# Gate and up of nine of eleven feature pairs by seven half-size products, and the down projection in four groups

## The chip, the cores and the metric

The kernel runs on one core of one Trainium2 chip. The metric is the device time of one execution in microseconds. Before the change it is 1094.81 us, the median of three runs (1094.68 to 1096.13). One execution was profiled as well; all rows below are from it.

The core has five engines with a queue of instructions each, worked off in order and tied together by semaphores: TensorE (PE in the rows, its weight loads PEld), VectorE (DVE), ScalarE (ACT), GpSimd (POOL) and SyncE (SP), which here only issues DMAs. SBUF is the working memory with 128 partitions, PSUM the matmuls' memory with eight banks.

## The reference

Two transformer layers over 512 tokens of width 1024, in float32. Layer A mixes tokens by a gated short convolution and attention to 256 memory tokens, layer B by sliding-window attention and the same memory. Each ends in a feed-forward part of width 2816:

```python
x = x + jnp.concatenate([y_tok, y_mem], axis=-1) @ w_out
h = rmsnorm(x, norm_ffn[i])
x = x + (jax.nn.silu(h @ w_gate[i]) * (h @ w_up[i])) @ w_down[i]
...
return rmsnorm(x, final_norm)
```

## The kernel before, in words

Features lie on the partitions, in blocks of 128: x has 8 blocks, the feed-forward 22, and a block spans all 512 tokens. Weights and activations are split into a high part (a cast on ScalarE, L95) and a low part (source minus high part on VectorE, L96), and `mm3` (L88 to L92) adds three matmuls, high by high, high by low and low by high. `project` (L320) makes one block of outputs from all blocks of inputs in one PSUM bank: 8 x 3 matmuls of 512 columns for gate or up, 22 x 3 for down.

Weights come in tiles of 128 x 1024 in the order of their use (`weight_order`), loaded on SP's queue and split two tiles ahead (`AHEAD`). Raw tiles have two buffers of their own, high and low parts three each, and the softmax tiles three; all other wide tiles share 31.

The feed-forward part (`ffn_up`, L543) goes through the 22 blocks: gate, 1/rms on VectorE (`times_r`, L278), Silu on ScalarE (L551), up, 1/rms, then the product of both on GpSimd (L555), and its split into h. `ffn_down` then makes the eight blocks of x from all 22 h; `residual` (L521) adds each to x and prepares the next norm. In layer B the last of the eight blocks is made by halves of the tokens (256 columns), so that one half is finished behind the other's products. The order on each engine is the order in which the code issues the work; small pieces of attention and norms are issued some steps later by `Background`.

Of the kernel before, what the change touches and what calls it, by code (L numbers as in the profile page):

```python
# [15 lines left out]
P = 128  # L16
D = 1024
# [19 lines left out]
NB = S // P  # L37

# blocks of the concatenated mixer outputs, in the order in which they appear
# [19 lines left out]
def yoco_kernel(ctx: ExitStack, tc: tile.TileContext, io: dict):  # L59
# [3 lines left out]
    wraw = ctx.enter_context(tc.tile_pool(name="wraw", bufs=2))  # L63
    wspl = ctx.enter_context(tc.tile_pool(name="wspl", bufs=3))
# [23 lines left out]
    def mm3(out, w, x, first, last):  # L88
        """out += w^T x from exact two-part splits; w, x = (hi, lo)."""
        nc.tensor.matmul(out, lhsT=w[0], rhs=x[0], start=first, stop=False)  # L90
        nc.tensor.matmul(out, lhsT=w[0], rhs=x[1], start=False, stop=False)  # L91
        nc.tensor.matmul(out, lhsT=w[1], rhs=x[0], start=False, stop=last)  # L92
# [30 lines left out]
    def weight_order():  # L123
        def mem_kv(i):
# [7 lines left out]
        def ffn(i):  # L132
            for f in range(KF):
                yield io["w_gate"][i, f]
                yield io["w_up"][i, f]
            for m in range(KD):
                for c in range(0, KF, 8):
                    yield io["w_down"][i, m][:, c * P:min(c + 8, KF) * P]
# [672 lines left out]
```

## Time and profile before

| | before |
|---|---|
| median of three runs | 1094.81 us |
| profiled execution, span from first to last instruction | 1092.4 us |
| TensorE, VectorE, ScalarE, GpSimd busy | 1075.7, 587.2, 423.7, 188.1 us |
| matmuls of 512 columns, of 256 columns | 4238, 628 |
| moved by DMA | 108.66 MB |

The page gives one execution's span and no time around it; the median of the runs is 2.4 us longer. Busy time counts the recorded duration of instructions. Matmuls are recorded from start to modelled end and overlap, so the distance from one start to the next is what a matmul takes of TensorE. The counts of matmuls are from the program's order, the rest from the page.

### The profile page before, as it was taken

What the parts mean: (1) busy time and instruction counts of PE and PEld (TensorE: products, weight loads), DVE (VectorE), ACT (ScalarE), POOL (GpSimd) and SP (SyncE); (2) the same over time, 40 slices, a digit from 0 to 9 for tenths busy, and PEclk for the clock granted to TensorE, in tenths of its full rate; (3) what the DMA queues carried; (4) which work ended last, traced back from release to release, by engine and by line L of the source; (5) the groups of instructions that cost most, each with busy time, mean ns of one, the idle gap of its engine ahead of it and who ended that gap; (6) DMA issues with size and microseconds to landing.
All of it is one profiled execution on the core that took longest, in us unless ns stands there. A gap on an engine that the chain in (4) does not pass through costs nothing. (4 is left out here: it accounts for less than half of the span.)

```text
span 1092.4 us, 13009 instructions
## 1 busy us (share of the span) xinstructions
PE 1075.7 (98%) x5152; PEld 902.2 (83%) x5152; DVE 587.2 (54%) x782; ACT 423.7 (39%) x700; POOL 188.1 (17%) x143
## 2 busy tenths in 40 slices
PE   9999999999999999999999999999999999999996
PEld 7788988888888888888888887888888888888886
DVE  7587856454545454333369798744545454532223
ACT  6346634332323232223258687543323233322220
POOL 5331202210101010000012133330101010100000
PEclk9999999999999999999999999999999999999998
DMA  7323233223232323333351222132232323233222
GB/s 224 125 97 115 77 127 106 89 86 110 86 111 84 111 86 102 87 98 100 105 174 59 92 63 70 44 130 96 82 112 85 108 89 105 89 95 105 88 87 77
DMA packets 34036, 108.66 MB, mean 99 GB/s; under 512 B 3852, under 2 KB 7864, under 8 KB 33848
## 3 DMA queue, kind: packets, MB, share of 16 engines
q1 hardware_dynamic: 31840, 103.82, 29.4%
q10 hardware_dynamic: 2136, 4.01, 1.3%
q8 instruction: 40, 0.66, 0.2%
q14 instruction: 20, 0.16, 0.1%
HBM read 105.71 MB, written 4.47 MB: 101 GB/s over the span
## 5 line engine op out<-in xcount | busy, mean ns | idle before, releaser
L95 ACT CAST whi<-raw 128x1024 fp32r<-128x1024 f32 (+2 forms) x196 | 199.4, 1018 | 508.5 <-PE p_u L91 168.6
L96 DVE TENSOR_TENSOR wlo<-raw,whi 128x1024 fp32r<-128x1024 f32 (+2 forms) x196 | 287.8, 1469 | 182.1 <-ACT whi L95 181.4
L555 POOL TENSOR_TENSOR fu<-fg,fu 128x512 f32<-128x512 f32 x44 | 58.1, 1320 | 412.2 <-ACT whi L95 268.5
L91 PE MATMUL p_d<-h,whi 128*128 128x512 f32 x330 | 128.4, 389 | 0.0
L90 PE MATMUL p_d<-h,whi 128*128 128x512 f32 x330 | 128.4, 389 | 0.0
L92 PE MATMUL p_d<-h,wlo 128*128 128x512 f32 x330 | 128.4, 389 | 0.0
L90 PEld LDWEIGHTS p_d<-h,whi 128*128 128x128 f32 x330 | 61.9, 188 | 13.0
L91 PEld LDWEIGHTS p_d<-h,whi 128*128 128x128 f32 x330 | 61.9, 188 | 12.9
L92 PEld LDWEIGHTS p_d<-h,wlo 128*128 128x128 f32 x330 | 61.9, 188 | 12.7
L90 PE MATMUL p_u<-xoa,whi 128*128 128x512 f32 x176 | 68.6, 390 | 0.0
L90 PE MATMUL p_u<-xob,whi 128*128 128x512 f32 x176 | 68.6, 390 | 0.0
L90 PE MATMUL p_g<-xoa,whi 128*128 128x512 f32 x176 | 68.5, 389 | 0.0
L90 PE MATMUL p_g<-xob,whi 128*128 128x512 f32 x176 | 68.5, 389 | 0.0
L92 PE MATMUL p_g<-xoa,wlo 128*128 128x512 f32 x176 | 68.5, 389 | 0.0
L92 PE MATMUL p_g<-xob,wlo 128*128 128x512 f32 x176 | 68.5, 389 | 0.0
L91 PE MATMUL p_g<-xoa,whi 128*128 128x512 f32 x176 | 68.5, 389 | 0.0
L91 PE MATMUL p_g<-xob,whi 128*128 128x512 f32 x176 | 68.5, 389 | 0.0
L92 PE MATMUL p_u<-xoa,wlo 128*128 128x512 f32 x176 | 68.5, 389 | 0.0
L92 PE MATMUL p_u<-xob,wlo 128*128 128x512 f32 x176 | 68.5, 389 | 0.0
L91 PE MATMUL p_u<-xoa,whi 128*128 128x512 f32 x176 | 68.5, 389 | 0.0
L91 PE MATMUL p_u<-xob,whi 128*128 128x512 f32 x176 | 68.5, 389 | 0.0
L278 DVE TENSOR_TENSOR fu<-p_u,rb_fb 128x512 f32<-128x512 f32 x22 | 15.2, 691 | 69.5 <-PE p_u L92 69.5
(321 smaller groups left out, 2079.0 us busy)
## 6 DMA issues: line engine op xcount, KB each, us to landing
raw<-in_w_gate SPq DMA_DIRECT2D x44, 512.0 KB, 3.5
raw<-in_w_up SPq DMA_DIRECT2D x44, 512.0 KB, 3.5
raw<-in_w_down SPq DMA_DIRECT2D x32, 512.0 KB, 3.5
raw<-in_a_w_in SPq DMA_DIRECT2D x14, 512.0 KB, 3.5
raw<-in_w_down SPq DMA_DIRECT2D x16, 384.0 KB, 3.1
raw<-in_a_w_out SPq DMA_DIRECT2D x8, 512.0 KB, 3.4
raw<-in_b_w_q SPq DMA_DIRECT2D x8, 512.0 KB, 3.5
raw<-in_b_w_out SPq DMA_DIRECT2D x8, 512.0 KB, 3.4
```

The costliest lines, as they stand in the source:

```text
L90: nc.tensor.matmul(out, lhsT=w[0], rhs=x[0], start=first, stop=False)
L91: nc.tensor.matmul(out, lhsT=w[0], rhs=x[1], start=False, stop=False)
L92: nc.tensor.matmul(out, lhsT=w[1], rhs=x[0], start=False, stop=last)
L95: nc.scalar.copy(out=hi, in_=src)
L96: nc.vector.tensor_tensor(out=lo, in0=src, in1=hi.bitcast(F32), op=ALU.subtract)
L278: nc.vector.tensor_tensor(out=t, in0=acc, in1=norm.row, op=ALU.mult)
L555: nc.gpsimd.tensor_tensor(out=u, in0=t, in1=u, op=ALU.mult)
```

## The change

Features are taken in pairs of blocks, eleven of them. Two pairs (`PLAIN`) are computed as before, except that VectorE instead of GpSimd multiplies gate and up. For the other nine, gate and up are one unit each: the product of [two output blocks x 1024 inputs] with [1024 inputs x 512 tokens] is cut into quarters (inputs in even and odd blocks, tokens in two halves of 256) and computed by seven products of quarter size for eight, in Winograd's form of Strassen's identity. Four of the seven weight operands are sums of quarters (t1 to t4), made by `minus`; four of the activations' are sums too (s1 to s4). `XForms` makes all activations' operands once per layer, after normalising x fully on VectorE, and splits them into high and low parts. `Unit` loads a unit's weights, makes and splits its operands and issues the products; partial sums leave PSUM by way of ScalarE copies (`self.r`) and VectorE additions (`evacuate`). For w11 and w21 the low part is made by ScalarE writing the negated high part and an accumulating DMA on GpSimd's queue adding the weights from DRAM to it.

`Queue` runs a clock of matmul times as the code is issued, and `work.at` puts every step of a unit at a time relative to its first product: the load 16 products ahead, and so on. The down projection is made in four groups of pairs (`SPLITS`), each added to x; the last group of layer B has its last two blocks by halves of the tokens. The buffers of raw and split weights and of the softmax move into one pool of 41 wide tiles (`DBUFS`). Comments are left out of the diff.

```diff
+DBUFS = 41
+PLAIN = 2
+SPLITS = ((0, 1), (2, 3, 4), (5, 6, 7), (8, 9, 10))
+def mm_time(n):
+    return n / 2400 + 0.0135
+SLOT = 3 * NJ * mm_time(H)
...
-        return slots.tile([P, 2, S], dt, tag="d", name=name, bufs=31)
+        return slots.tile([P, 2, S], dt, tag="d", name=name, bufs=DBUFS)
...
     def probs(name):
-        """Softmax tile, [queries, block of queries, 256 keys]."""
-        t = slots.tile([P, 2, S], F32, tag="p", name=name, bufs=3)
+        t = wide(name, F32)
...
+        def pump(self):
+            while self.items and self.items[0][0] <= self.now:
+                heapq.heappop(self.items)[2]()
...
+    def mm3(out, w, x, first, last, reopen=False):
+        work.now += 3 * mm_time(out.shape[-1])
+        nc.tensor.matmul(out, lhsT=w[0], rhs=x[0], start=first, stop=False, skip_group_check=reopen)
+        nc.tensor.matmul(out, lhsT=w[0], rhs=x[1], start=False, stop=False, skip_group_check=reopen)
+        nc.tensor.matmul(out, lhsT=w[1], rhs=x[0], start=False, stop=last, skip_group_check=reopen)
...
+        def down(i, s):
+            k0, k1 = 2 * SPLITS[s][0], 2 * SPLITS[s][-1] + 2
+            yield from (io["w_down"][i, m][:, k0 * P:k1 * P] for m in range(KD))
...
+            raw, hi, lo = (wide(f"{t}{n}", dt).rearrange("p a b -> p (a b)")[:, :w]
+                           for t, dt in (("raw", F32), ("whi", FR), ("wlo", FR)))
...
+    XFORM = {1: "x11", 2: "x12", 3: "s4", 4: "x22", 5: "s1", 6: "s2", 7: "s3"}
+    WFORM = {1: "w11", 2: "w21", 3: "w22", 4: "t4", 5: "t1", 6: "t2", 7: "t3"}
...
+        def group(self, jj):
+            d = {}
...
+            def normed(k):
+                if k % 4 == 0:
+                    d["e"], d["o"] = (wide(f"xn{self.name}{c}{jj}", F32) for c in "eo")
+                nc.vector.scalar_tensor_tensor(out=d["eo"[k % 2]][:, k % 4 // 2, :], in0=x[k], scalar=gain(self.g, k),
+                                               in1=self.norm.row, op0=ALU.mult, op1=ALU.mult)
+                self.normed += 1
...
+            def combine(out, a, b, op):
...
+                nc.vector.tensor_tensor(out=d[out], in0=d[a], in1=d[b], op=op)
...
+            def divide(f):
+                t = wide(f"xf{self.name}{f}{jj}")
+                hi, lo = (t[:, z, :].rearrange("p (k t) -> p k t", t=H) for z in range(2))
+                split(d[f], hi, lo)
+                self.t[f, jj] = t
...
+            yield from (lambda k=k: normed(k) for k in range(4 * jj, 4 * jj + 4))
+            yield lambda: divide("x11")
+            yield lambda: combine("s1", "x21", "x22", ALU.add)
+            yield lambda: combine("s2", "s1", "x11", ALU.subtract)
+            yield lambda: divide("x12")
+            yield lambda: combine("s3", "x11", "x21", ALU.subtract)
+            yield lambda: combine("s4", "x12", "s2", ALU.subtract)
+            yield from (lambda f=f: divide(f) for f in ("s2", "s1", "s3", "x22", "s4"))
...
+            def load():
+                for c in range(2):
+                    d[c] = flat(f"raw{name}{c}", F32)
+                    nc.sync.dma_start(out=d[c], in_=src[:, 2 * c * W:2 * (c + 1) * W])
...
+            def plain():
+                hi, lo = flat(f"hi{name}a", FR), flat(f"lo{name}a", FR)
+                nc.scalar.copy(out=hi, in_=d[0])
+                nc.scalar.activation(lo, hi.bitcast(F32), AF.Copy, scale=-1.0)
+                nc.gpsimd.dma_start(out=lo, in_=src[:, :2 * W], accum_op=ALU.add)
+                halves(hi, lo, ("w11", "w21"))
...
+            def w22():
+                t = wide(f"w22{name}")
+                self.w["w22"] = t[:, 0, :], t[:, 1, :]
+                split(d["w22"], *self.w["w22"])
...
+            def minus(out, a, b):
+                nc.vector.tensor_tensor(out=d[out], in0=d[a], in1=d[b], op=ALU.subtract)
...
+            def high(c):
+                d["hi", c] = flat(f"hi{name}t{c}", FR)
+                nc.scalar.copy(out=d["hi", c], in_=d[c])
+            def low(c, names):
+                lo = flat(f"lo{name}t{c}", FR)
+                nc.vector.tensor_tensor(out=lo, in0=d[c], in1=d["hi", c].bitcast(F32), op=ALU.subtract)
+                halves(d["hi", c], lo, names)
...
+            for slot_, fn in (
+                    (-16, load), (-8, plain), (-6.5, w22), (-5.5, lambda: minus("w12", "w12", "w11")),
+                    (-5, lambda: minus("w22", "w22", "w12")), (-4, lambda: high(1)),
+                    (-3, lambda: low(1, ("t2", "t1"))), (-1.5, lambda: minus("w11", "w22", "w11")),
+                    (-1, lambda: minus("w21", "w21", "w22")), (0, lambda: high(0)),
+                    (1, lambda: low(0, ("t3", "t4")))):
+                work.at(t0 + slot_ * SLOT, fn)
...
+        def product(self, k, xf):
...
+            b = {1: "a", 6: "a", 7: "a", 4: "a", 2: "b", 5: "c", 3: "c"}[k]
+            opens = k in (1, 2, 5)
+            if opens:
+                self.bank[b] = ps(f"{b}{self.name}")[:, :H]
+            for j in range(NJ):
+                w = tuple(t[:, j * P:(j + 1) * P] for t in self.w[f])
+                mm3(self.bank[b], w, xf.part(XFORM[k], j), opens and j == 0, j == NJ - 1,
+                    not opens)
+                work.pump()
+            self.done.add(k)
+            if k in (1, 6, 7):
+                self.r[k] = slot(f"r{k}{self.name}", F32, H)
+                nc.scalar.copy(out=self.r[k], in_=self.bank["a"])
+            if k == 2:
+                self.evacuate(0, 0, self.bank["b"], self.r[1])
+            if k == 4:
+                self.evacuate(0, 1, self.bank["a"], None)
+            if k in (5, 7) and {5, 7} <= self.done:
+                self.evacuate(1, 1, self.bank["c"], self.r[7])
+            if k == 3:
+                self.evacuate(1, 0, self.bank["c"], self.r[6])
+            bg.tick()
...
+        def gate(f, e, bank, r):
+            to = quarter(g, f, e)
+            def silu(src):
+                nc.scalar.activation(to, src, AF.Silu)
+                gated.add((f, e))
+            if r is None:
+                silu(bank)
+                return
+            nc.vector.tensor_tensor(out=to, in0=bank, in1=r, op=ALU.add)
+            work.after(0.9, lambda: silu(to))
...
+        def up(f, e, bank, r):
+            work.until(lambda: (f, e) in gated)
+            to, by = quarter(u, f, e), quarter(g, f, e)
+            if r is not None:
+                nc.vector.tensor_tensor(out=to, in0=bank, in1=r, op=ALU.add)
+                bank = to
+            nc.vector.tensor_tensor(out=to, in0=bank, in1=by, op=ALU.mult)
+            count[f] += 1
+            if count[f] == 2:
+                hi, lo = pair_of(f"h{i}_{2 * p + f}")
+                work.after(0.8, lambda: nc.scalar.copy(out=hi, in_=u[:, f, :]))
...
+                def low():
+                    nc.vector.tensor_tensor(out=lo, in0=u[:, f, :], in1=hi.bitcast(F32), op=ALU.subtract)
+                    h[2 * p + f] = hi, lo
+                work.after(1.6, low)
...
+        count = [0, 0]
+        return [Unit(io["w_gate4"][i, p - PLAIN], t0, f"g{i}_{p}", gate),
+                Unit(io["w_up4"][i, p - PLAIN], t0 + 7 * SLOT, f"u{i}_{p}", up)]
...
+    def down(h, blocks, name):
+        early = len(blocks) - 2
+        acc, w = [], []
+        for m in range(2):
+            w.append(next(weights))
+            acc.append(ps(f"{name}{m}"))
+            for k in range(early):
+                mm3(acc[m], cols(w[m], k), h[blocks[k]], k == 0, False)
+                work.pump()
+                if k % 2:
+                    bg.tick()
+        work.until(lambda: all(b in h for b in blocks))
+        for m in range(2):
+            for k in range(early, len(blocks)):
+                mm3(acc[m], cols(w[m], k), h[blocks[k]], k == 0, k == len(blocks) - 1)
+            work.pump()
+            bg.tick()
+            yield m, acc[m]
+        for m in range(2, KD):
+            yield m, project([h[b] for b in blocks], f"{name}{m}", len(blocks))
...
+    def ffn(i, xg, norm, g):
...
+        for s in range(1, len(SPLITS)):
+            work.at(downs[s] - 7, weights.open)
+            for n, p in enumerate(SPLITS[s]):
+                units[p] = ffn_units(i, p, starts[s] + 14 * n * SLOT, h)
...
+        for f in range(2 * PLAIN):
             pg = project(xg, f"g{i}_{f}")
...
-            nc.gpsimd.tensor_tensor(out=u, in0=t, in1=u, op=ALU.mult)
+            if f == 0:
+                xf = XForms(norm, g, f"{i}", 1.25)
+            nc.vector.tensor_tensor(out=u, in0=t, in1=u, op=ALU.mult)
             hi, lo = pair_of(f"h{i}_{f}")
             split(u, hi, lo)
-            h.append((hi, lo))
+            h[f] = hi, lo
...
+        for s in range(len(SPLITS)):
+            prev = None
+            todo = [u for p in SPLITS[s] if p >= PLAIN for u in units[p]]
+            for u in todo:
+                order = [(u, 1), (u, 2), (prev, 4), (u, 6), (prev, 3)]
+                order += [(u, 7), (u, 5), (u, 4), (u, 3)] if u is todo[-1] else [(u, 5), (u, 7)]
+                for v, k in order:
+                    if v is not None:
+                        v.product(k, xf)
+                prev = u
+            if s < len(SPLITS) - 1:
+                work.until(lambda: xf.normed == KD)
+                for m, acc in down(h, blocks_of(s), f"d{i}{s}_"):
+                    nc.vector.tensor_tensor(out=x[m], in0=acc, in1=x[m], op=ALU.add)
+                for b in blocks_of(s):
+                    del h[b]
         return h
...
-    def ffn_down(i, h, norm, g):
-        return [residual(m, project(h, f"d{i}_{m}", KF), norm, g, f"xd{i}") for m in range(KD)]
...
+    LAST = len(SPLITS) - 1
...
+    h = ffn(0, xg, nF, G_FFN0)
...
+    xg = [residual(m, acc, nB, G_MIX1, "xd0") for m, acc in down(h, blocks_of(LAST), "d0_")]
...
+    w = {m: next(weights) for m in (KD - 2, KD - 1)}
+    blocks = blocks_of(LAST)
+    for t0 in (0, H):
+        for m in (KD - 2, KD - 1):
+            acc = ps(f"d1_{m}_{t0}")[:, :H]
+            for n, b in enumerate(blocks):
+                mm3(acc, cols(w[m], n), tuple(a[:, t0:t0 + H] for a in h[b]), n == 0, n == len(blocks) - 1)
...
```

Three places of the order. The first is VectorE in the gate and up products of layer A, in the kernel before (block 18 to 19: `fg` and `fu` are gate and up after 1/rms, `wlo` a weight tile's low part, `h` the low part of h).

```order
L278 TENSOR_TENSOR fg_18_3107<-p_g_18_3076,rb_fa 128x512
L96 TENSOR_TENSOR wlo_3113<-raw_3111,whi_3112 128x1024
L278 TENSOR_TENSOR fu_18_3141<-p_u_18_3110,rb_fa 128x512
L96 TENSOR_TENSOR wlo_3150<-raw_3148,whi_3149 128x1024
L96 TENSOR_TENSOR h_18_3144<-fu_18_3141,h_18_3144 128x512
L278 TENSOR_TENSOR fg_19_3178<-p_g_19_3147,rb_fa 128x512
L96 TENSOR_TENSOR wlo_3184<-raw_3182,whi_3183 128x1024
L278 TENSOR_TENSOR fu_19_3212<-p_u_19_3181,rb_fa 128x512
L96 TENSOR_TENSOR wlo_3221<-raw_3219,whi_3220 128x1024
L96 TENSOR_TENSOR h_19_3215<-fu_19_3212,h_19_3215 128x512
```

The same place in the change, where pair 9 follows pair 8 (`rawg`, `rawu` are weights in which sums are made in place, `log`, `lou` low parts, `g`, `u` the evacuated quarters, `r7`, `r1` partial sums that ScalarE copied).

```order
L761 TENSOR_TENSOR g_9_1793<-cg_9_4586,r7g_9_4617 128x256
L697 TENSOR_TENSOR rawg_101_4497<-rawg_101_4497,rawg_100_4495 128x512
L768 TENSOR_TENSOR u_9_1794<-bu_9_4641,r1u_9_4639 128x256
L770 TENSOR_TENSOR u_9_1794<-u_9_1794,g_9_1793 128x256
L705 TENSOR_TENSOR lou_9t_4683<-rawu_90_4370,hiu_9t_4665 128x1024
L135 TENSOR_TENSOR w22g_10_4673<-rawg_101_4497,w22g_10_4673 128x512
L697 TENSOR_TENSOR rawu_101_4626<-rawu_101_4626,rawu_100_4624 128x512
L697 TENSOR_TENSOR rawg_101_4497<-rawg_101_4497 128x512
L761 TENSOR_TENSOR g_9_1793<-cg_9_4586,r6g_9_4567 128x256
L697 TENSOR_TENSOR rawg_100_4495<-rawg_101_4497,rawg_100_4495 128x512
L697 TENSOR_TENSOR rawg_100_4495<-rawg_100_4495,rawg_101_4497 128x512
L705 TENSOR_TENSOR log_10t_4730<-rawg_101_4497,hig_10t_4715 128x1024
```

Two weight splits, two scalings and the split of h per block have become, per unit, four sums of weights, three splits and the additions and multiplications of quarters, interleaved by their times.

The second place is TensorE where one block of outputs follows another, before (from up of block 3 to gate of block 4 in layer A; the waits are those that the program writes down).

```order
L91 MATMUL p_u0_3_2045<-xoa_7_1779,whi45_1976 128x512
L92 MATMUL p_u0_3_2045<-xoa_7_1779,wlo45_1977 128x512
L90 MATMUL p_g0_4_2082<-xoa_0_1608,whi46_2013 128x512 [waits Activation_49]
L91 MATMUL p_g0_4_2082<-xoa_0_1608,whi46_2013 128x512
L92 MATMUL p_g0_4_2082<-xoa_0_1608,wlo46_2014 128x512 [waits DVE_49]
L90 MATMUL p_g0_4_2082<-xoa_1_1613,whi46_2013 128x512
L91 MATMUL p_g0_4_2082<-xoa_1_1613,whi46_2013 128x512
```

In the change, where the gate unit of pair 4 begins (`au0_3` is a bank of the up unit of pair 3, `ag0_4` of the gate unit of pair 4, `xf` an operand of the activations).

```order
L129 MATMUL au0_3_2680<-xf0s31_2168,hiu0_3t0_2725 128x256
L130 MATMUL au0_3_2680<-xf0s31_2168,hiu0_3t0_2725 128x256
L131 MATMUL au0_3_2680<-xf0s31_2168,lou0_3t0_2743 128x256
L129 MATMUL ag0_4_2805<-xf0x110_1918,hig0_4a_2706 128x256
L130 MATMUL ag0_4_2805<-xf0x110_1918,hig0_4a_2706 128x256
L131 MATMUL ag0_4_2805<-xf0x110_1918,log0_4a_2707 128x256 [waits DMASW4_49]
L129 MATMUL ag0_4_2805<-xf0x110_1918,hig0_4a_2706 128x256
L130 MATMUL ag0_4_2805<-xf0x110_1918,hig0_4a_2706 128x256
```

The bank's first product waits at its third matmul for a DMA of GpSimd's queue (DMASW), where before a weight tile's cast and subtraction were waited for.

The third place is TensorE at the end of the plain pairs in layer A, before at the last h block of the down projection (`h0_21`, after 63 matmuls of that block of outputs).

```order
L90 MATMUL p_d0_0_3363<-h0_20_3286,whi84_3365 128x512
L91 MATMUL p_d0_0_3363<-h0_20_3286,whi84_3365 128x512
L92 MATMUL p_d0_0_3363<-h0_20_3286,wlo84_3366 128x512
L90 MATMUL p_d0_0_3363<-h0_21_3357,whi84_3365 128x512 [waits Activation_49]
L91 MATMUL p_d0_0_3363<-h0_21_3357,whi84_3365 128x512 [waits DVE_49]
L92 MATMUL p_d0_0_3363<-h0_21_3357,wlo84_3366 128x512
```

In the change the first group has four h blocks, and the last of them (`h0_3`) comes after 18 matmuls on the others.

```order
L129 MATMUL d00_1_2177<-h0_2_2058,whi47_2104 128x512
L130 MATMUL d00_1_2177<-h0_2_2058,whi47_2104 128x512
L131 MATMUL d00_1_2177<-h0_2_2058,wlo47_2105 128x512
L129 MATMUL d00_0_2161<-h0_3_2152,whi46_2063 128x512 [waits Activation_49]
L129 MATMUL d00_1_2177<-h0_3_2152,whi47_2104 128x512
L130 MATMUL d00_0_2161<-h0_3_2152,whi46_2063 128x512 [waits DVE_49]
L131 MATMUL d00_0_2161<-h0_3_2152,wlo46_2064 128x512
L130 MATMUL d00_1_2177<-h0_3_2152,whi47_2104 128x512
L131 MATMUL d00_1_2177<-h0_3_2152,wlo47_2105 128x512
```

The wait for the last h block, for ScalarE's high part and VectorE's low part, stands 18 matmuls after the last up product instead of 63.

## Rows read from the trace of the kernel before

**Rows 1.** The page: span, busy engines, TensorE and its granted clock in 40 slices.

```profile
span 1092.4 us, 13009 instructions
PE 1075.7 (98%) x5152; PEld 902.2 (83%) x5152; DVE 587.2 (54%) x782; ACT 423.7 (39%) x700; POOL 188.1 (17%) x143
...
PE   9999999999999999999999999999999999999996
...
PEclk9999999999999999999999999999999999999998
```

**Rows 2.** Table of stretches: us, busy of each engine (instructions), granted clock, DMA.

```profile
60.00:190.00 130.00, 130.00 (x696) 112.51 (x695) 94.16 (x131) 66.89 (x123) 28.37 (x17) 1.00 0.33 109
190.00:435.00 245.00, 245.00 (x1088) 202.95 (x1088) 122.17 (x114) 76.29 (x94) 32.65 (x24) 1.00 0.29 95
435.00:560.00 125.00, 125.00 (x553) 103.05 (x552) 40.99 (x45) 36.31 (x45) 10.85 (x8) 1.00 0.33 98
560.00:720.00 160.00, 154.53 (x885) 132.63 (x884) 132.91 (x286) 113.18 (x270) 46.80 (x36) 1.00 0.28 91
720.00:960.00 240.00, 240.00 (x1066) 198.89 (x1065) 119.59 (x111) 74.33 (x91) 30.87 (x23) 1.00 0.29 95
```

**Rows 3.** Waits of TensorE, longest in total first: us, times, longest.

```profile
PE v L90 <- DVE kf L278: 1.7, 1, 1.7
PE pt_s L325 <- DVE den_s L650: 1.1, 1, 1.1
```

**Rows 4.** Timeline of TensorE, feed-forward of layer A: start, duration, instruction.

```profile
300.95 0.39 PE L90 MATMUL p_u<-xoa,whi 128*128 128x512 f32 x1
...
306.39 0.39 PE L90 MATMUL p_g<-xoa,whi 128*128 128x512 f32 x1
```

**Rows 5.** Timeline of TensorE in the last block, and that stretch's row.

```profile
1075.72 0.28 PE L90 MATMUL d<-h,whi 128*128 128x256 f32 x1
...
1079.20 0.28 PE L92 MATMUL d<-h,wlo 128*128 128x256 f32 x1
...
1069.50:1079.30 9.80, 9.80 (x84) 9.80 (x83) 0.42 (x1) 0.42 (x1) 0.00 (x0) 1.00 0.01 2
```

**Rows 6.** Timeline of VectorE, feed-forward of layer A; in brackets the idle time before.

```profile
307.50 2.33 DVE L96 TENSOR_TENSOR wlo<-raw,whi 128x1024 fp32r<-128x1024 f32 x1 [0.21 <-ACT whi L95]
309.75 0.68 DVE L96 TENSOR_TENSOR h<-fu,h 128x512 fp32r<-128x512 f32 x1
312.03 0.69 DVE L278 TENSOR_TENSOR fg<-p_g,rb_fa 128x512 f32<-128x512 f32 x1 [1.60 <-PE p_g L92]
312.94 1.22 DVE L96 TENSOR_TENSOR wlo<-raw,whi 128x1024 fp32r<-128x1024 f32 x1 [0.21 <-ACT whi L95]
...
432.62 1.23 DVE L96 TENSOR_TENSOR wlo<-raw,whi 128x1024 fp32r<-128x1024 f32 x1 [0.21 <-ACT whi L95]
433.76 0.68 DVE L96 TENSOR_TENSOR h<-fu,h 128x512 fp32r<-128x512 f32 x1
```

**Rows 7.** Groups of VectorE by form: count, busy us, mean ns, idle before.

```profile
L422 DVE TENSOR_TENSOR mem<-mem,rb_m 128x256 f32<-128x256 f32 x8 | 2.8, 413 | 0.0
L713 DVE TENSOR_TENSOR x<-d,x 128x256 f32<-128x256 f32 x2 | 0.8, 424 | 11.3 <-PE d L92 11.3
```

**Rows 8.** Groups of ScalarE by form.

```profile
L95 ACT CAST whi<-raw 128x1024 fp32r<-128x1024 f32 x170 | 179.0, 1053 | 451.8 <-PE p_u L91 164.8 <-PE p_d L91 118.7 <-PE p_g L91 100.5
L95 ACT CAST h<-fu 128x512 fp32r<-128x512 f32 x44 | 27.4, 624 | 58.3 <-POOL fu L555 58.3
L228 ACT ACTIVATE sq_m<-mem 128x256 f32<-128x256 f32 x7 | 2.4, 404 | 0.4 <-DMA mem<-in_memT 0.4
```

**Rows 9.** Timeline of GpSimd beside the first of rows 6.

```profile
307.45 1.29 POOL L555 TENSOR_TENSOR fu<-fg,fu 128x512 f32<-128x512 f32 x1 [9.59 <-DVE fu L278]
```

**Rows 10.** The page: queue of the loads (packets, MB, share), one issue (KB, us).

```profile
q1 hardware_dynamic: 31840, 103.82, 29.4%
...
raw<-in_w_gate SPq DMA_DIRECT2D x44, 512.0 KB, 3.5
```

**Rows 11.** Timeline of VectorE at the end of the kernel.

```profile
1082.57 0.42 DVE L713 TENSOR_TENSOR x<-d,x 128x256 f32<-128x256 f32 x1 [2.10 <-PE d L92]
```

**Rows 12.** What VectorE waited for before a weight tile's low part: us, times.

```profile
  ACT whi L95: 181.4, 143
```

More of the change, by code (lines that the diff above doesn't have):

```diff
@@ L1 @@
+import heapq
 import math
@@ L86, in ps, with __init__, at, after @@
         return psum.tile([P, 512], F32, tag="ps", name=name)
[L88 to L92, printed above, removed]
+    class Queue:
+        def __init__(self):
+            self.now, self.n, self.items = 0.0, 0, []
+        def at(self, t, fn):
+            self.n += 1
+            heapq.heappush(self.items, (t, self.n, fn))
+        def after(self, dt, fn):
+            self.at(self.now + dt, fn)
+        def pump(self):
+            while self.items and self.items[0][0] <= self.now:
+                heapq.heappop(self.items)[2]()
+        def until(self, done):
+            while not done():
+                heapq.heappop(self.items)[2]()
+    work = Queue()
+    def mm3(out, w, x, first, last, reopen=False):
[3 more added lines that the diff above has]
+        nc.tensor.matmul(out, lhsT=w[1], rhs=x[0], start=False, stop=last, skip_group_check=reopen)
     def split(src, hi, lo):
@@ new lines, in part_b @@
+        def part_b():
+            yield from (io["b_w_q"][NCH + m] for m in range(2))
+            yield from (io["w_k"][m] for m in range(2))
+            yield from (io["w_v"][c] for c in range(2))
+            yield from (io["b_w_q"][m] for m in range(NCH))
+            yield from out(io["b_w_out0"], io["b_w_out"])
+        phase = 0
+        for i, part in enumerate((part_a, part_b)):
+            for group in (part(), plain_ffn(i), down(i, 0)):
+                yield from ((phase, w) for w in group)
+            for s in range(1, len(SPLITS)):
+                phase += 1
+                yield from ((phase, w) for w in down(i, s))
@@ new lines, in yoco_kernel, with __init__, load, fill @@
+    class Weights:
+        def __init__(self):
+            self.todo, self.ready, self.phase, self.n = list(weight_order()), [], 0, 0
+        def load(self):
+            n, src = self.n, self.todo.pop(0)[1]
+            self.n += 1
+            w = src.shape[-1]
+            raw, hi, lo = (wide(f"{t}{n}", dt).rearrange("p a b -> p (a b)")[:, :w]
+                           for t, dt in (("raw", F32), ("whi", FR), ("wlo", FR)))
+            step = 256 if n == 0 else w
+            for c in range(0, w, step):
+                nc.sync.dma_start(out=raw[:, c:c + step], in_=src[:, c:c + step])
+                split(raw[:, c:c + step], hi[:, c:c + step], lo[:, c:c + step])
+            self.ready.append((hi, lo))
+        def fill(self):
+            while self.todo and self.todo[0][0] <= self.phase and len(self.ready) <= AHEAD:
+                self.load()
+        def open(self):
+            self.phase += 1
+            self.fill()
+        def __next__(self):
+            self.fill()
+            return self.ready.pop(0)
@@ L181, in cols @@
+    weights = Weights()
     def cols(w, k, n=P):
@@ new lines, in blocks_of @@
+    def blocks_of(s):
+        return [b for p in SPLITS[s] for b in (2 * p, 2 * p + 1)]
+    def ffn(i, xg, norm, g):
+        t, starts, downs = work.now, [], []
+        block = 3 * KD * mm_time(S)
+        for pairs in SPLITS:
+            starts.append(t)
+            t += sum(4 * block if p < PLAIN else 14 * SLOT for p in pairs)
+            downs.append(t)
+            t += 2 * len(pairs) * block
+        h, units = {}, {}
+        for s in range(1, len(SPLITS)):
+            work.at(downs[s] - 7, weights.open)
+            for n, p in enumerate(SPLITS[s]):
+                units[p] = ffn_units(i, p, starts[s] + 14 * n * SLOT, h)
+        xf = None
+        for f in range(2 * PLAIN):
@@ L682, in yoco_kernel @@
     xg = out_proj(ORDER_B, nF, G_FFN1, "ob")
-    h = ffn_up(1, xg, nF)
+    h = ffn(1, xg, nF, G_FFN1)
     nE = Norm("e", split_last=True)
-    for m in range(KD - 1):
-        acc = project(h, f"d1_{m}", KF)
+    products = down(h, blocks_of(LAST), "d1_")
+    for m in range(KD - 2):
+        _, acc = next(products)
         nc.vector.tensor_tensor(out=x[m], in0=acc, in1=x[m], op=ALU.add)
         nE.add(x[m], m)
-    m, H = KD - 1, S // 2
     def output(t0, c):
```

141 lines of the change are left out of this document (68 added, 73 removed).

## Prediction

> **What bounds the kernel now.** I read the page first. TensorE is busy 1075.7 of 1092.4 us, its digit is 9 in 39 of 40 slices, and its clock is granted in full until the last slice [rows 1]. The table of stretches then says where the rest can matter: in the first feed-forward part (190 to 435 us) and the second (720 to 960 us) TensorE is busy all the time, while VectorE works half of it and ScalarE less than a third [rows 2]. The waits of TensorE confirm it: the longest is 1.7 us, and none stands in the feed-forward [rows 3]. So the time is the sum of the matmuls' spacings, and any change is priced first in matmuls. The duration printed for a matmul (0.39 us) is no price, since it overlaps the next; I take starts. Between the first matmul of p_u and the first of the next p_g lie 24 matmuls of 512 columns in 5.44 us, 0.2267 us each [rows 4]. In the last block of the down projection stand 30 matmuls of 256 columns in a row, 29 steps in 3.48 us, 0.1200 us each [rows 5]. Two halves thus cost 0.2400 us against 0.2267 for a whole; this surcharge is what the change must beat. There the weight loads are already busy all the time (9.80 of 9.80 us) and the spacing still holds [rows 5].
>
> The Trainium skill (TensorE: Matmul & The Clock Gate, section "Back-to-back issue gap") gives an isolated gap of columns over 2.4 GHz plus 2.5 ns: 109.2 ns for 256 columns and 215.8 for 512. The trace does not agree: its spacings have 13.3 to 13.4 ns beyond the columns, not 2.5. By the page the first term below would be an estimated 36 x (84 x 0.1092 - 48 x 0.2158) = -42.7 us.
>
> **The change part by part.**
>
> *Products.* A unit is gate or up of one feature pair: 36 units in two layers. Before, 2 blocks x 8 x 3 = 48 matmuls of 512 columns, 10.88 us. After, 7 products x 4 x 3 = 84 of 256 columns, 10.08 us. Saved: 0.80 us each, 28.8 in all. The last part of the kernel now has two blocks by halves over six feature blocks instead of one over 22: 30 matmuls of 512 more, 60 of 256 fewer, -0.4 us. Sum of the PE terms: **-29.2 us**. The down projection keeps its products in the other groups; its sums go to x four times instead of once, 48 more VectorE additions of 0.69 us [rows 6]. They lie behind products in stretches where VectorE is about half idle [rows 2], and cost nothing unless VectorE is late there by more than a block of 18 matmuls, 4.1 us.
>
> *VectorE and ScalarE beside the new units.* Durations: on VectorE 1.22 us for 1024 columns, 0.68 for 512, 0.42 for 256 [rows 6, 7]; on ScalarE 1.05, 0.62 and 0.40 [rows 8]. VectorE per unit: five subtractions of 512 columns and two of 1024, 5.84 us. Per pair come ten operations of 256 (six sums, four multiplications) and two of 512: 2 x 5.84 + 4.2 + 1.36 = 17.2 us in 20.16 us of products, 85%. The durations overlap the next start by 0.09 us (an operation of 1.23 us is followed after 1.14) [rows 6], so in spacings it is 15.0 us, 75%. ScalarE: per unit four of 1024, one of 512 and three copies of 256, per pair four Silu of 256 and two casts: 14.9 us, 74%. Both fit, but TensorE now waits on chains through them: a partial product must be copied out before the next is added to the same bank. In the order two other products (2.88 us) stand between each such pair inside a unit's regular run, and the split parts of the weights are due five products or more before their use. What that costs the trace of before bounds by two stretches: with VectorE busy 72% and ScalarE 51% (60 to 190 us) TensorE lost nothing; with 83% and 71% (560 to 720) it lost 5.5 of 160 us, of which 1.7 is one wait for a whole key projection that has no counterpart here [rows 2, 3], so 2.4%. On 18 x 20.16 = 363 us that is 0 to 8.6 us. The new share, 75 to 85%, lies between the rows; I take half, **+4.4 us**.
>
> *The plain pairs and the first group of the down projection.* The two pairs that stay whole give VectorE 2 x 1.22 + 2 x 0.69 + 2 x 0.68 = 5.18 us per 10.88 (the multiplication comes over from GpSimd; where that now runs, VectorE's 1.22 us becomes 2.33 [rows 6, 9], so this removes a collision). From the second block on, the 30 steps of the transformed inputs are added, 0.68 us every 1.25 us: 5.92 more, 11.1 of 10.88 us by durations, 9.9 or so by spacings. VectorE is at its limit for 32 us and may end 0 to 4 us late. The group's last h passes VectorE 0.69, VectorE 0.68, ScalarE 0.62, VectorE 0.68 and three handovers of 0.21 [rows 6, 8]: 3.3 us. Ahead of it the order puts 18 matmuls, 4.1 us. Before, 63 matmuls covered the same chain. So each layer waits 0 to 3 us; I take 1: **+2 us**. Later groups have 24 matmuls (5.4 us) ahead of a chain of 2 x 0.42 + 0.62 + 0.68 and handovers, 2.8 us: nothing.
>
> *The accumulating transfer.* The low part of w11 and w21 is no longer a subtraction: ScalarE writes the negated high part, and a DMA on GpSimd's queue adds the weights to it. The first product's third matmul waits for that. Two ScalarE operations (2.1 us) and the DMA are placed 8 products, 11.5 us, ahead, so 9.4 us are left. No row shows such a DMA. From below, a plain load of the same 512 KB lands after 3.5 us [rows 10]; from above, twice that, since the destination is read too, 7.0 us. Load on the engines: 103.82 MB took 29.4% of them over the span [rows 10], 3.1 us per MB; a unit moves 1.05 MB plainly and about as much for the accumulation, 6.5 of 10.08 us. Both ends are hidden; I take 0. GpSimd's queue has only these DMAs in that stretch, so nothing else is held.
>
> *One pool of SBUF tiles.* 41 wide tiles instead of 31 beside eleven other buffers. A load now waits for whatever tile it reuses. In the order the plain high and low parts of a unit take tiles that TensorE releases 11.8 us or more ahead of their use (from the spacings of rows 4 and 5), and raw weights are loaded 16 products ahead. 0, between -1 and +2.
>
> *Sum.* Span 1092.4 - 29.2 + 4.4 + 2 = 1069.6 us. The page gives the span alone; the median of the runs, 1094.81, is 2.4 us above it, and I leave that as it is: **1072 us**. The tail after the last product, 9.8 us [rows 11], keeps its chain.
>
> **Rivals.**
>
> *A. No new waits.* The low ends of all terms: 1094.8 - 29.2 = 1065.6 us. For it: TensorE lost nothing in the stretch at 72%. Against: two layers with VectorE at its limit for 32 us.
>
> *B. VectorE takes over.* It works in order, and before each split it stood idle for ScalarE's high part: 181.4 us over 143 waits, 1.27 each [rows 12]. A unit has three such splits, a pair six: 7.6 us. If none is filled, a pair takes 17.2 + 7.6 = 24.8 us on VectorE against 20.16 on TensorE: 18 x 4.6 = 84 us more, 1150 us. It decides from 2.9 us of idle time per pair; from 4.6 us on the kernel is slower than before. Against: those waits stood where VectorE had nothing else to do; now other operations of the same unit stand between the cast and the subtraction in the order. A partial form, a third of the waits (2.5 us a pair), still costs nothing.
>
> *C. The accumulating DMA is late.* Every microsecond by which it takes more than 9.4 us is paid 36 times, since each unit's issue hangs on the run of products before. It makes the kernel slower from (29.2 - 6.4) / 36 = 0.6 us on, a landing of 10.0 us; at 11 us the time is 1072 + 58 = 1130 us. For it: VectorE and GpSimd exclude each other when both work on SBUF (1.22 us becomes 2.33 beside a GpSimd operation of 1.29 [rows 6, 9]), and VectorE will be 75 to 85% busy; if making the transfer's descriptors has to wait for gaps several times over, several 1.22 us add up. Against: one such delay, 7.0 + 1.2, still fits. The Trainium skill (SBUF — State Buffer, section "SBUF: two separate sides") has this as a trap: a DMA of GpSimd's queue needs descriptors written by GpSimd's cores, which are locked out while VectorE runs in a mode of two ports. By the same section VectorE with two SBUF inputs contends only with a GpSimd instruction that reads SBUF, so the trap need not close here. The trace agrees on the exclusion (1.22 against 2.33 us); no run here shows it for descriptors.
>
> *D. A tie.* Waits of 27 to 31 us, for instance 1.6 us per pair, bring 1092.6 to 1097.0.
>
> **How the numbers follow.** Forecast with its own range 1067 to 1082: 0.54. Rival A, 1064 to 1067: 0.15. A partial B or C, 1082 to 1092.6: 0.11. D: 0.04. Slower: C 0.10, B 0.06. What a measurement of this kernel can tell from no change is about 0.2%, 2.2 us; so faster 0.80, same 0.04, slower 0.16. For 8 in 10 I leave out at most the slower cases and the edge of D: 1064 to 1092.
>
> **What would show it.** Spacing of 0.120 us in the new products and none of the units longer than 10.3 us: the PE term. In the waits of TensorE: first products of a unit waiting for a DMA of GpSimd's queue speak for C; products waiting for VectorE's low parts throughout for B; a wait at the first matmul on the fourth h block for the third term. The new DMA's time to landing should be 3.5 to 7 us. I am wrong if the time lies under 1064 (then the rest of the kernel has changed as well) or if the waits in the new stretches exceed 27 us.

## The result and the profile after

The changed kernel takes 1171.21 us (median of 4 runs, 1167.93 to 1175.43) against 1094.74 before: ratio 1.0694, interval [1.0668, 1.072]. I had forecast 1072. The profiled execution has a span of 1170.6 us, 78.2 more than before.

The page of the changed kernel, to be read beside [rows 1]:

```profile
span 1170.6 us, 16345 instructions
PE 1078.5 (92%) x6418; PEld 951.5 (81%) x6418; DVE 738.8 (63%) x1203; ACT 560.8 (48%) x997; POOL 159.5 (14%) x136
PE   7988989997899989989997989899789998998997
PEclk9999999999999999999998999999999999998999
PE 56%; issue 16%; DVE 8%; DMA 6%; ACT 5%; POOL 0%; ACTq 0%; DVEq 0%; POOLq 0%
```

TensorE now idles 92.1 us instead of 16.7, and the digits below 9 begin in the first slices, long before the first new product. So I cut both traces at the first product of each part (first p_g, first product of each down group, first product of a unit, first product after the last down group) and subtracted. The columns behind "after" are versions of the experiments below, "best" the fastest of them.

| part, us | before | after | one pool alone | own tiles 33 | VectorE low | own 34 + VectorE low | best |
|---|---|---|---|---|---|---|---|
| first mixer | 196.2 | 222.3 | 222.5 | 196.9 | 223.5 | 196.2 | 196.8 |
| plain pairs + first down group, layer A | - | 76.0 | - | 66.7 | 76.0 | 66.8 | 66.8 |
| three unit stretches, A | - | 200.9 | - | 193.8 | 183.9 | 183.3 | 182.8 |
| second mixer | 163.4 | 185.1 | 183.5 | 170.7 | 183.3 | 170.8 | 164.8 |
| plain pairs + first down group, layer B | - | 76.0 | - | 66.8 | 76.0 | 66.8 | 66.8 |
| three unit stretches, B | - | 202.5 | - | 183.2 | 183.9 | 181.5 | 181.4 |

The other down groups last 32.7 us in every version that has them, which is 8 x 18 products at 0.2267. A unit stretch without waits lasts 60.5 us: 504 products of 256 columns at 0.120. The 78.2 us are therefore 47.9 in the two mixers, of which no product was changed; 18.4 in the plain pairs and first groups (76.0 against 66.8, twice); 40.6 in the unit stretches (403.5 against 6 x 60.48); less 28.7, the remainder, for the products.

Waits of TensorE after the change, in a first down group (262 to 300 us) and in the last unit stretch (1056 to 1127 us): engine, line, releaser, us in all, times, longest.

```profile
PE p_d L131 <- DVE wlo L135: 6.0, 5, 1.7
...
PE au L131 <- DMA lou_8a<-in_w_up: 3.3, 1, 3.3
PE ag L131 <- DMA log_9a<-in_w_gate: 1.5, 1, 1.5
PE au L131 <- DMA lou_9a<-in_w_up: 1.1, 1, 1.1
```

The new waits are for low parts of streamed weights, and for the accumulating DMA. Neither engine nor DMA is busy enough to explain them. The DMA queue's own waits over the whole run say where to look:

```profile
SPq L219 <- DVE wlo L135: 111.8, 21, 15.6
SPq L675 <- PE p_d L131: 97.6, 17, 10.9
```

L219 issues the streamed weights, L675 the units' loads; both wait for other work to give back a tile of the pool. That such a wait costs time does not follow from its length. The kernel before, where TensorE idles 16.7 us in all, has far more of them on its own two raw tiles:

```profile
SPq L168 <- DVE wlo L96: 905.0, 187, 15.9
```

So the pool is a suspicion here, and the runs have to decide.

### The profile page after: what moved, and what is told of

The parts are those of the page before. It is cut to its first block, busy times and chain, and to the rows that moved or that the text cites. A ratio compares the mean times of both kernels' runs of the same rounds, so it can differ in the third digit from the quotient of the medians.

```text
span 1170.6 us, 16345 instructions
## 1 busy us (share of the span) xinstructions
PE 1078.5 (92%) x6418; PEld 951.5 (81%) x6418; DVE 738.8 (63%) x1203; ACT 560.8 (48%) x997; POOL 159.5 (14%) x136
## 4 chain that ended last, share of the span: by engine, by line
PE 56%; issue 16%; DVE 8%; DMA 6%; ACT 5%; POOL 0%; ACTq 0%; DVEq 0%; POOLq 0%
PE p_d L131 3%; PE p_d L129 3%; PE p_d L130 3%; PE au L131 2%; PE au L129 2%; PE au L130 2%; PE ag L131 2%; PE d L130 2%; PE d L131 2%; PE d L129 2%; PE ag L129 2%; PE ag L130 2%; DVE wlo L135 2%; DMA lou_2a<-in_w_up 1%; PE p_g L131 1%
## 5 line engine op out<-in xcount | busy, mean ns | idle before, releaser
L135 DVE TENSOR_TENSOR wlo<-raw,whi 128x1024 fp32r<-128x1024 f32 (+3 forms) x140 | 152.1, 1091 | 25.6 <-ACT whi L134 23.1
L134 ACT CAST whi<-raw 128x1024 fp32r<-128x1024 f32 (+3 forms) x140 | 123.7, 898 | 45.7 <-DMA raw<-in_w_down 35.4
L130 PE MATMUL p_d<-h,whi 128*128 128x512 f32 x252 | 98.2, 390 | 0.0
L129 PE MATMUL p_d<-h,whi 128*128 128x512 f32 x252 | 98.1, 389 | 0.0
L131 PEld LDWEIGHTS p_d<-h,wlo 128*128 128x128 f32 x252 | 47.3, 188 | 25.8 <-DVE wlo L135 16.2
L130 PEld LDWEIGHTS p_d<-h,whi 128*128 128x128 f32 x252 | 47.3, 188 | 10.0
L129 PEld LDWEIGHTS p_d<-h,whi 128*128 128x128 f32 x252 | 47.3, 188 | 9.5
L130 PE MATMUL d<-h,whi 128*128 128x512 f32 (+1 forms) x112 | 41.3, 369 | 2.5 <-DVE h L135 2.5
L131 PE MATMUL p_cv<-xa,wlo 128*128 128x512 f32 x96 | 38.5, 401 | 4.8 <-DVE wlo L135 4.8
L131 PE MATMUL d<-h,wlo 128*128 128x512 f32 (+1 forms) x112 | 41.3, 368 | 0.8 <-DVE wlo L135 0.8
L129 PE MATMUL p_cv<-xa,whi 128*128 128x512 f32 x96 | 39.0, 407 | 2.4 <-ACT whi L134 1.7
L129 PE MATMUL d<-h,whi 128*128 128x512 f32 (+1 forms) x112 | 40.9, 368 | 0.0
L130 PE MATMUL p_cv<-xa,whi 128*128 128x512 f32 x96 | 38.0, 396 | 0.0
L697 DVE TENSOR_TENSOR rawu<-rawu,rawu 128x512 f32<-128x512 f32 x54 | 37.0, 684 | 0.2
L697 DVE TENSOR_TENSOR rawg<-rawg,rawg 128x512 f32<-128x512 f32 x54 | 35.8, 685 | 0.3
L755 ACT ACTIVATE g<-g 128x256 f32<-128x256 f32 x54 | 22.6, 418 | 25.3 <-DVE g L761 24.6
```

The costliest lines, as they stand in the source:

```text
L134: nc.scalar.copy(out=hi, in_=src)
L135: nc.vector.tensor_tensor(out=lo, in0=src, in1=hi.bitcast(F32), op=ALU.subtract)
L697: nc.vector.tensor_tensor(out=d[out], in0=d[a], in1=d[b], op=ALU.subtract)
L755: nc.scalar.activation(to, src, AF.Silu)
```

## The experiments

Theory P blames the one pool. Tiles are handed out in the order in which the program asks, so a weight tile queues behind activation tiles. Its rival Q: the mixers lose to something else. Theory C: the accumulating DMA is late. Its rival V: VectorE can't take its place.

**One pool alone**, put into the kernel before:

```
-    wraw / wspl / tag "p" tiles (2, 3, 3 and 3)
+    raw, hi, lo and probs from wide(), bufs=41
```

> The kernel before with one part of the change alone: raw, high and low weight tiles and softmax tiles come from one pool of 41 wide tiles. No Strassen product, no accumulating DMA. Between equal points of the two traces the changed kernel lost 26.1 us in the first mixer and 21.7 us in the second, 47.8 us, although no product of the mixers changed. Theory P (one pool: a weight tile is handed out only after the activation tiles that the program asks for ahead of it, so its cast and its low part stand behind theirs in ScalarE's and VectorE's queues): the mixers lose the 48 us here too and the FFNs, which have few activation tiles, 0 to 5: 1140 to 1150 us. Rival Q (the mixers lose them to something else of the change, such as the larger program or a lower clock that the new products bring): within 3 us of the 1094.7 before.

1141.24 us, ratio 1.0418 [1.0401, 1.0434]. The mixers lose 26.3 and 20.0 us; the feed-forward parts keep their 240.8 and 119.8 us. P holds. How it happens shows on ScalarE; first the kernel before, then this one (start, duration; in brackets the idle time ahead and its releaser):

```profile
45.27 1.04 ACT L95 CAST whi<-raw 128x1024 fp32r<-128x1024 f32 x1 [5.34 <-PE p_cv L91]
46.22 0.58 ACT L256 COPY rb_a<-rb_a 128x512 f32<-128x512 f32 x1
50.75 0.72 ACT L471 ACTIVATE c<-u,small 128x512 f32<-128x512 f32 x1 [3.96 <-POOL u L469]
52.56 0.72 ACT L471 ACTIVATE c<-u,small 128x512 f32<-128x512 f32 x1 [1.09 <-POOL u L469]
53.19 1.04 ACT L95 CAST whi<-raw 128x1024 fp32r<-128x1024 f32 x1
55.71 0.62 ACT L95 CAST yc<-b 128x512 fp32r<-128x512 f32 x1 [1.47 <-POOL b L475]
```

```profile
61.93 0.62 ACT L93 CAST yc<-b 128x512 fp32r<-128x512 f32 x1 [2.43 <-POOL b L472]
62.93 0.37 ACT L253 COPY rb_m<-rb_m 128x256 f32<-128x256 f32 x1 [0.38 <-PE rb_m L249]
65.41 0.62 ACT L93 CAST yc<-b 128x512 fp32r<-128x512 f32 x1 [2.10 <-POOL b L472]
65.93 1.04 ACT L93 CAST whi<-raw 128x1024 fp32r<-128x1024 f32 x1
```

Before, two weight casts stand ahead of the first yc; here the next cast stands behind both, which wait for GpSimd. The text ahead of the prediction says that each engine works in the order in which the code issues the work. These lines show that this is not exact: the code issues the first yc before the second c, and the edit moves no line that issues a cast. In the built program the order moved with the tiles. TensorE's waits of this run in its first mixer:

```profile
PE p_cv L90 <- DVE wlo L94: 4.7, 3, 2.8
PE p_cv L88 <- ACT whi L93: 1.4, 1, 1.4
```

The order of casts is not the whole loss of the first mixer. At the start of the kernel SyncE now asks for four blocks of x ahead of the first weights instead of one, and the first p_cv comes 7.2 us later (first the kernel before, then this one):

```profile
0.73 0.40 SPq L487 DMA_DIRECT2D x<-in_xT  x1
1.18 1.37 SPq L165 DMA_DIRECT2D raw<-in_a_w  x3
38.90 0.39 PE L90 MATMUL p_cv<-xa,whi 128*128 128x512 f32 x1
```

```profile
0.73 1.81 SPq L484 DMA_DIRECT2D x<-in_xT  x4
2.58 1.99 SPq L162 DMA_DIRECT2D raw<-in_a_w  x3
46.05 0.39 PE L88 MATMUL p_cv<-xa,whi 128*128 128x512 f32 x1
```

The other 19.2 us are lost behind it.

**Own tiles for the streamed weights**, in the changed kernel:

```
-DBUFS = 41
+DBUFS = 33
-raw, hi, lo = (wide(...))
+raw, hi, lo = (slots.tile(tag=t, bufs=b)) with b = 2, 3, 3
```

> The changed kernel, with its 41 wide tiles divided again: raw 2, high 3 and low 3 tiles of the streamed weights under names of their own, 33 for everything else (units included). Theory P: the 47.8 us of the mixers return, and of the first down groups (29.3 us each for products of 21.8 us at the spacing of 0.2267 us) up to 7.5 us each: 1108 to 1125 us. Rival Q: no change, 1165 to 1175 us. A third outcome, that the units starve on 33 tiles, would show as loads of the units waiting for products and as Strassen stretches longer than the 65 to 70 us they have now, at mixers as long as before.

1087.43 us, 0.993 [0.9915, 0.9945]: the same 41 tiles, only divided, and 84 us gone. It is more than P gave, because the unit stretches returned 26.5 us as well: TensorE's waits on the accumulating DMA fell from 25.8 to 7.9 us, and in the second and third unit stretch of layer B none is left.

**VectorE's low part**, pool as changed:

```
-nc.scalar.activation(lo, hi, Copy, scale=-1.0); nc.gpsimd.dma_start(out=lo, accum_op=ALU.add)
+nc.vector.tensor_tensor(out=lo, in0=d[0], in1=hi, op=ALU.subtract)
```

> The changed kernel, with the low part of w11 and w21 made by one VectorE subtraction of 128x1024 instead of ScalarE's negated copy and the accumulating DMA; the pool stays. Theory C (the accumulating DMA comes late: TensorE's waits for it are 25.8 us in the trace, with some more for the lower clock behind a wait): 1130 to 1148 us. Rival V (VectorE, with 36 more subtractions of about 1.1 us, becomes the bound beside the units): the waits on DMA give way to waits on VectorE's low parts of the same size, 1160 to 1180 us. Both leave the mixers as slow as they are.

1137.15 us, 1.0384 [1.0369, 1.04]. C holds and V falls: four of six unit stretches stand at 60.5 us.

**Both edits**, 34 tiles for the rest:

> Both edits, with 34 tiles for everything but the streamed weights (42 in all). Theories P and C together: 1171 less 48 for the mixers, less up to 15 for the first down groups, less 26 to 40 for the accumulating DMA: 1070 to 1097 us. Under Q and V: 1160 to 1180 us. Under P and V: 1108 to 1125 us.

1073.35 us, 0.980 [0.9783, 0.9816], as P and C say. The second mixer still has 7.4 us too many.

**Order or shortage?** Two runs. The first has the pool of 41 and `AHEAD = 4`, the second the own tiles, VectorE's low part and `DBUFS = 30`:

> The changed kernel, one pool of 41, with streamed weights asked for four tiles ahead of their use instead of two. It tells two readings of the pool apart. Order (a tile's cast stands behind the activations that the program asks for first, so that the lead of two tiles is too short): two products of 2.7 to 5.4 us more of lead cover waits of 1 to 3 us each, the mixers and first down groups return most of their 48 and 15 us, and the waits on the accumulating DMA stay: 1110 to 1135 us. Shortage (41 tiles are too few): six tiles more are held by weights, all parts become slower: above 1175 us.

> As the run with 34 tiles beside the streamed weights' own eight and VectorE's low part (1073.35 us), but with 30: 38 wide tiles in all, three fewer than the changed kernel has. Order: the number matters little, within 6 us of 1073. Shortage: mixers slower by tens of us, 1100 us or more.

The first took 1158.21 us (1.0576 [1.056, 1.0591]), between my two cases: the first mixer regains half (208.7) and the first groups most (24.3 instead of 29.2), the second mixer (189.9) and the unit stretches (411.7 in all) lose. Cut at the first p_cv, the first mixer says more: its start loses 11.4 us against the kernel before (6.8 in the changed kernel), but behind it only 1.1 us are lost instead of 19.4. There the longer lead, in the same 41 tiles, removes nearly all of the loss. The second took 1091.79 (0.9956 [0.994, 0.9972]), also between: its mixers are untouched at 197.1 and 170.6 with 38 tiles in all, and its unit stretches in layer A rise to 65.2, 66.1 and 65.5. So the first mixer suffers from order, the units from shortage; the second mixer lost more with the longer lead and returned only with tiles divided again. In that run's layer A (240 to 329 us) the units' loads wait for unit tiles, at most 23.5 us where it was 15.2 with 34 tiles:

```profile
SPq L675 <- DVE lou_4t L704: 23.5, 1, 23.5
```

**Softmax tiles.** As the run with both edits, but with three tiles of their own for softmax and 31 for the rest:

> As the run with 34 tiles, but softmax tiles get three of their own again and 31 are left (42 in all, as before the change). The second mixer took 170.8 us there against 163.4 us before. Theory S (softmax tiles are handed out behind activation tiles): it returns to 163 to 165 us, 1066 to 1068 us in all. Rival T (the last down group delivers a block of x every 4.1 us, where the down projection before delivered one every 15 us, so the eight blocks' scaled copies are still being made when the second mixer wants them): the second mixer stays at 170 us, 1072 to 1075 us in all.

1082.49 us, 0.9879 [0.9864, 0.9894]. Theory S holds for the second mixer (163.3), and the units pay: 62.3 to 64.4 us a stretch. The total was a miss, since I had not counted the three tiles taken from them.

**Units' loads and accumulating DMA 2.5 slots earlier**, with 33 tiles: `(-18.5, load), (-10.5, plain)`.

> The run with the streamed weights' own tiles and the accumulating DMA (1087.43 us), with the units' loads 2.5 slots (3.6 us) earlier, at -18.5, and the high part, negated copy and accumulating DMA 2.5 slots earlier, at -10.5. Its six Strassen stretches took 65.0, 64.7, 64.1, 62.2, 60.5 and 60.5 us; 60.5 is what 504 products at 0.120 us take. Theory C (the accumulating DMA only starts too late): all six come to 60.5 to 61.5 us, 1074 to 1078 us in all. Rival (33 tiles don't give the units their loads earlier, or the DMA is slowed by other transfers wherever it stands): no gain, 1084 us or more.

1086.46 us, 0.9923 [0.9906, 0.9939]: no gain. Asked for earlier, the units' loads in layer A wait for tiles as before (at most 21.6 us, 19.7 without the edit), and the stretches stay at 63.0 to 66.1 us: to ask earlier doesn't help where no tile is free.

**A division that serves both**: softmax 3, weights 2 + 3 + 3, 31 for the rest, and each unit's w22 from the softmax tiles, empty at that time; with VectorE's low part, with the accumulating DMA, and with VectorE's low part and loads at -13:

```
-t = wide(f"w22{name}")
+t = slots.tile([P, 2, S], FR, tag="p", name=f"w22{name}", bufs=3)
```

> Own tiles for the streamed weights (2, 3, 3), three for softmax, 31 for the rest, VectorE's low part; as the run that took 1082.49 us, but each unit's w22 takes its tile from the softmax tiles' three, which stand empty beside the units. There the mixers were as before (196.5 and 163.3 us), and the six Strassen stretches took 62.3 to 64.4 us instead of 60.5. Shortage beside the units (31 tiles hold up the units' loads): with two to three tiles relieved the stretches come to 60.5 to 62 us, 1064 to 1072 us in all. Rival (three tiles for w22 hold each unit's w22 until the unit two before is done, a new wait): no gain, 1080 us or more.

> The same division of tiles, with ScalarE's negated copy and the accumulating DMA kept. In the changed kernel the accumulating DMA started 2.0 to 8.3 us before the first product on its tile, where the forecast had 9.4 us; in the second layer of the run with 33 tiles it started 7.0 to 10.1 us before it and nothing waited in two of three stretches. Theory L (its start is late only because tiles come late): within 6 us of the run with VectorE's low part, 1066 to 1077 us. Rival C (it is late wherever tiles are given): 1085 us or more.

> As the first of this set, with the units' loads at -13 slots instead of -16 (4.3 us later), which holds two raw tiles of each unit for three slots less. Shortage: the same or up to 4 us faster than the first. Rival (the loads are then late: 4.5 us to land, high part wanted 7.2 us later): waits on raw tiles, 3 us or more slower.

1067.36 us (0.9743 [0.9727, 0.9759]), 1080.86 (0.9872 [0.9855, 0.9889]) and 1069.09 (0.9761 [0.9746, 0.9776]). The first is the fastest. The second lies between L and C: in layer B two stretches stand at 60.5 us with the accumulating DMA, in layer A all are late (67.0, 62.7, 62.8). The third gains nothing. The first's page:

```profile
span 1067.1 us, 16240 instructions
PE 1050.0 (98%) x6418; PEld 942.1 (88%) x6418; DVE 783.5 (73%) x1239; ACT 537.6 (50%) x961; POOL 131.1 (12%) x100
PE   9999999999999999999999999999999999999996
PE 38%; DVE 1%; DVEq 0%; issue 0%
```

The chain of waits, which the page follows back over 39% of the span here as before, is products again. VectorE is busy 73% and late nowhere for more than 1.8 us.

## Why the prediction was wrong

*The step that failed* is "One pool of SBUF tiles ... 0, between -1 and +2". Measured alone it costs 46.5 us (1141.24 - 1094.74); in the changed kernel, dividing the tiles again returned 83.8, of which 39.8 in the mixers. I had looked at when a reused tile is released, in the unit stretches only, and that is not what decides in the mixers: [rows 2, 3] show these as the part with the least slack, and I priced no change there because no line of them changed. Yet the order of the casts around the first yc, which can be read from the built programs without a run, had moved.

*The accumulating transfer, 0.* My bound on its landing, 3.5 to 7.0 us, was nearly right: 5.4 to 6.4 us for 28 of 36, 7.1 to 9.0 for the other eight, all with a unit's load moving beside them. Wrong were the 9.4 us left for it, twice over.

First, in the order of products. The code places the steps of a group's units as if each began seven products, 10.1 us, behind the one before. But the first unit leaves two of its seven products (4 and 3) to be done later, so every further unit begins two products, 2.9 us, earlier than its steps assume. In a stretch without waits of the best version the first products of three units stand 7.2 and 10.1 us apart, where the placing has 10.1 twice:

```profile
962.41 0.28 PE L129 MATMUL ag<-xf1x,hig_8a 128*128 128x256 f32 x1
969.60 0.28 PE L129 MATMUL au<-xf1x,hiu_8a 128*128 128x256 f32 x1
979.68 0.28 PE L129 MATMUL ag<-xf1x,hig_9a 128*128 128x256 f32 x1
```

The transfer of five units in six is thus placed 6 products ahead, 8.6 us, of which ScalarE's two operations leave 6.5 us and not 9.4: enough for the 28, not for the eight. No run moved the steps by just these two products; the run with 2.5 slots more gained nothing, at 33 tiles.

Second, the steps come later than they are placed. Changed kernel, the way to one such DMA, in order of time (start, duration; in brackets the idle time ahead and its releaser):

```profile
1052.61 0.69 DVE L855 TENSOR_TENSOR x<-p_d,x 128x512 f32<-128x512 f32 x1 [1.92 <-PE p_d L131]
1053.21 0.69 DVE L135 TENSOR_TENSOR w22g<-rawg,w22g 128x512 fp32r<-128x512 f32 x1
1053.93 0.69 DVE L697 TENSOR_TENSOR rawg<-rawg 128x512 f32<-128x512 f32 x1
...
1054.71 1.06 ACT L701 CAST hig_8t<-rawg 128x1024 fp32r<-128x1024 f32 x1 [15.57 <-DVE rawg L697]
1055.67 1.05 ACT L686 CAST hiu_8a<-rawu 128x1024 fp32r<-128x1024 f32 x1
1058.60 0.37 ACT L731 COPY r1g<-ag 128x256 f32<-128x256 f32 x1 [1.88 <-PE ag L131]
1058.87 1.06 ACT L687 ACTIVATE lou_8a<-hiu_8a 128x1024 fp32r<-128x1024 f32 x1
...
1060.22 0.86 POOL L688 DMA_DIRECT2D lou_8a<-in_w_up  x1 [20.43 <-ACT lou_8a L687]
...
1062.24 0.28 PE L129 MATMUL au<-xf1x,hiu_8a 128*128 128x256 f32 x1
1067.64 0.58 PE L131 MATMUL au<-xf1x,lou_8a 128*128 128x256 f32 x1 [3.32 <-DMA lou_8a<-in_w_up]
```

The up unit's raw tiles were asked for at 1027.0 and 1030.6 us. But its cast and its negated copy stand on ScalarE behind the gate unit's cast, which waits 15.6 us for differences that VectorE makes only after an addition to x of the down group; the copy then stands behind r1g, which waits for a product. Units' and down group's tiles come from one pool, and in the program's order the units' take those that the down weights give back. So the DMA starts 2.0 us before the first product on its tile; over all 36 units of the changed kernel it is 2.0 to 8.3 us, but for those a whole down group ahead. With own tiles 33, layer B, it starts 7.0 us or more before, 8.3 in the unit shown, and nothing waits for it:

```profile
1000.16 0.86 POOL L688 DMA_DIRECT2D lou_9a<-in_w_up  x1 [11.02 <-PE ag L131]
...
1008.42 0.28 PE L129 MATMUL au<-xf1x,hiu_9a 128*128 128x256 f32 x1
1008.66 0.28 PE L131 MATMUL au<-xf1x,lou_9a 128*128 128x256 f32 x1
```

So rival C came true by another cause than the descriptors I named: its issue on GpSimd took 0.86 to 0.88 us, and 1.06 and 0.93 for the first of each layer. C was not paid 36 times either; TensorE's 15 waits for it sum to 25.8 us.

*Plain pairs and first group, +2.* They lost 18.4 us in the changed kernel, but with own tiles they take 66.7 us a layer without a wait, of which 21.8 are the group's 96 products at 0.2267: the term is 0. The wait I expected, on the last h, is 1.3 us per layer in the changed kernel and gone with own tiles; the waits on low parts of the down weights (6.0 us) came from the pool.

*VectorE beside the units, +4.4.* Too high: with 36 more subtractions on VectorE four stretches run at 60.5 us. Rival B fell.

*Products, -29.2.* Right: 0.120 us a product, and in the best version 25.3 us off the span, with 2.1 us back in the mixers and 1.4 in the unit stretches. *Tail, 0:* right, 10.0 us instead of 9.8.

Why the units of layer A need more than those of layer B stays open. Layer A also holds the second mixer's memory keys and values, three wide tiles; with 30 to 33 shared tiles its three stretches together are slower than those of B in every run (by 13.7 us with 30, by 0.1 in the run with loads at -13), which fits, but no run took these tiles away. In the run with softmax tiles of their own, layer B had 62.3 to 62.6 us too, against 60.6 to 61.8 with 30, so the number of tiles alone is not the whole of it. Nor was the crowded start (first product at 7.14 instead of 4.80 us, 6.8 us at the first p_cv) tried apart from the order.

## What to carry to other kernels

Merging pools is a change of order, not only of room: if tiles are handed out in the program's order, a stream that used to run ahead (weights) is tied to whatever is asked for first, also where no line was edited. Compare the order of casts and loads in the stages with the least slack before pricing the merge at nothing, and give each stream its own few tiles; lend idle ones (here the softmax tiles) to a stage that needs them. A lead placed in slots is worth only what the order of products and the tile's release leave of it: count it from the first product as it is really ordered.

## What the hardware showed

A wait can cost more than its length. In the changed kernel, behind a wait of 2.0 us, the second mixer's key projection steps at 0.43 us instead of 0.2267, which is the lower granted level (1.2 GHz), and the mean granted clock of 612 to 618 us is 0.72. Other waits did no such thing: around the one of 1.5 us that ended at 1082.0 us, before a low part of pair 9's gate, the clock of 1080 to 1086 us is 1.00.

```profile
614.09 0.63 PE L130 MATMUL p_k<-xkv,whi 128*128 128x512 f32 x1
614.52 0.63 PE L131 MATMUL p_k<-xkv,wlo 128*128 128x512 f32 x1
...
612.00:618.00 6.00, 5.47 (x24) 4.32 (x25) 2.38 (x5) 2.73 (x4) 0.00 (x0) 0.72 0.17 46
```

Steps between two products of one width that lie within 4% of the lower level's 0.427 and 0.213 us, with no wait between them, number 84 in the changed kernel and cost 10.4 us above the two spacings; before there are none. And an accumulating DMA of 512 KB takes 1.6 times as long as a plain load (5.6 to 5.9 against 3.5 us [rows 10]) in the six cases of the changed kernel in which no other load moves beside it.
